# Twenty of the first FFN's 22 up tiles as seven half-width products, with the residual in DRAM and five queues in written order

## The chip, the cores and the metric

The kernel runs on one core of a Trainium2 chip. A core has five engines that each work through a queue of their own: TensorE (PE, matrix products; its loads of the stationary operand are listed apart as PEld), VectorE (DVE), ScalarE (ACT), GpSimd (POOL) and SyncE (SP, which here only issues DMA transfers; POOL issues some too). Working data lies in SBUF, results of matmuls in PSUM, inputs in DRAM. The metric is the device time of one execution in microseconds, as the median of several.

## The reference

Two layers of a transformer block. Layer 0 has a Fourier/Hyena mixer, layer 1 attention; both end in a convolutional FFN. Layer 0 works on 512 tokens x and on 256 context tokens ctx.

```python
def _conv_ffn(h, w_up, conv_w, conv_b, w_down):
    gate, val = jnp.split(h @ w_up, 2, axis=-1)          # h: tokens x 1024, w_up: 1024 x 5632
    return (jax.nn.silu(_dwconv3(gate, conv_w, conv_b)) * val) @ w_down   # 2816 -> 1024
...
x = x + g1 * yx                                          # yx: the mixer's output
x = x + g2 * _conv_ffn(_modulate(_rms_norm(x, norm2[i]), sh2, sc2), *ffn)
ctx = ctx + cg1 * yc
ctx = ctx + cg2 * _conv_ffn(_modulate(_rms_norm(ctx, norm2[i]), csh2, csc2), *ffn)
```

`_dwconv3` is a convolution of three taps along the tokens. The gains `g2`, shifts and scales come from `silu(c) @ w_mod + b_mod`, a vector by matrix product for each of the conditions.

## The kernel before

Features lie on the 128 partitions and tokens along the free axis. Targets and context stand side by side in one row of 772 columns: 512 targets, two zeros, 256 context tokens, two zeros, so that one convolution runs over both. A vector of 1024 features is eight such tiles. To keep float32 accuracy each operand is split into a rounded part and a rest, and each product is three matmuls (`mm3`, L194 to L198): high by high, high by rest, rest by high. ACT makes the high part (`hi`, L171), DVE subtracts it to give the rest (`lo`, L176). Weights come as 128 x 1024 tiles into the three buffers `wr` by SP's DMA and are split into `wh` and `wl`.

The first FFN is `ffn` (L1194 to L1251). The 2816 inner features are 22 tiles f. For each tile, `up(f)` loads a gate and a value weight, and runs 8 k tiles x 2 x 3 matmuls over 512 columns and as many over 260: 96 matmuls in all. Then come the convolution (`conv3`, L419 to L421, one ACT and two DVE operations), Silu (L1221), the product with the value half (L1223) and a split into `ah` and `al`. `fill` puts three of the vector by matrix products behind each tile from the third on (`gemv_dve`, a DVE multiply and sum of 128 x 1024, L282, and a small one, L283); 56 of them, with 80 DVE steps in all, fill DVE's free time in this FFN. The down product runs in groups of 8, 8 and 6 tiles (`GROUPS`), each by `res_proj` (L1148 on): eight output tiles m, each a sum over the group's k tiles, added to the residual `x` in SBUF by a DVE operation that scales it by the gain (L1189). The last group runs in two stages: first all eight m over the 512 target columns, then over the 260 others. The pieces of layer 1's first norm hang on these steps (`norm_hook`, L371): while the second stage runs on PE, DVE and ACT make the squares (L313) of the target columns, PE folds them over the partitions (L319) and spreads the result, and DVE and ACT scale the tiles. Layer 1's first product follows. An automatic scheduler orders this FFN on the engines.

Layer 1's FFN (`ffn_blocks`, L1795) already runs most of its tiles by Strassen's scheme: the k axis is halved and the columns are halved, so that gate and value tiles become a 2 x 2 block product done with seven products of half width, on sums of weight blocks (tiles `sum`, made by POOL DMAs, plain at L1872 and accumulating at L1874, and by DVE at L1878 and L1881). A table of step names, `UP_ORDER`, is the order of its queues. Each of its two sums has two buffers.

## Time and profile before

| | us |
|---|---|
| median of 3 runs | 1619.88 (1616.86 to 1622.33) |
| the profiled execution, its own time | 1611.81 |
| its span | 1610.0 |
| first FFN, from 377.00 to the last group's second stage at 917.85 | 540.85 |
| layer 1's FFN, 1262 to 1609 | 347 |

The mean granted TensorE clock of the profiled execution is 0.991. Rows of windows give, after the stretch and its length, the busy time and number of instructions of PE, PEld, DVE, ACT and POOL, then the granted clock, the mean busy share of the 16 DMA engines and GB/s. Rows of groups give line, engine, operation, output and inputs by the program's names, shape and count, then busy time and mean ns of one, then the engine's idle time before them and what ended it. Rows of the timeline give start, duration, engine and operation. A matmul's row is longer than the distance to the next start, since matmuls overlap in the array; the distance is what counts.

### The profile page before, as it was taken

The numbers are of one execution on the slowest core, as the hardware profiler recorded it, in microseconds if no ns is written. First come the engines' busy times: TensorE is split into PE (matmuls) and PEld (weight loads), VectorE is DVE, ScalarE is ACT, GpSimd is POOL, SyncE is SP. The second block draws the span as 40 slices with busy tenths as digits, with TensorE's granted clock in tenths as the row PEclk, the third lists the DMA queues.
The fourth block names the chain that finished last, engine by engine and source line by source line (L and its number), as shares of the span: only waits on it lengthen the run. The fifth ranks groups of instructions, "written<-read, shape, count | busy, mean of one in ns | idle before, by whom it ended". The sixth has DMA issues, their size and how long they took to land.

```text
span 1610.0 us, 22860 instructions
## 1 busy us (share of the span) xinstructions
PE 1560.5 (97%) x8968; PEld 1312.2 (82%) x8968; DVE 1173.2 (73%) x1963; ACT 671.8 (42%) x980; POOL 166.3 (10%) x245
## 2 busy tenths in 40 slices
PE   7999998999999999999999999999999999999998
PEld 5787887888888888888888887666648899999897
DVE  6789969878887354553354475799996899788784
ACT  4441234434232212321123244998883664444441
POOL 0022134000000000000000000122230022121110
PEclk9999999999999999999999998999999999999999
DMA  9336512533544244442343220000006266665543
GB/s 359 108 116 213 170 34 81 188 118 106 163 156 139 66 131 142 140 150 66 102 139 100 102 69 20 1 24 14 1 27 209 92 155 169 155 155 145 147 125 105
DMA packets 68121, 189.23 MB, mean 118 GB/s; under 512 B 7979, under 2 KB 15341, under 8 KB 66989
## 3 DMA queue, kind: packets, MB, share of 16 engines
q1 hardware_dynamic: 59053, 166.79, 31.6%
q0 software_dynamic: 8960, 20.98, 6.2%
q8 instruction: 70, 1.15, 0.3%
q14 instruction: 38, 0.31, 0.1%
HBM read 181.97 MB, written 5.77 MB: 117 GB/s over the span
## 4 chain that ended last, share of the span: by engine, by line
PE 76%; DVE 16%; issue 2%; ACT 2%; DMA 2%; POOL 1%; SPq 0%; DVEq 0%; ACTq 0%; POOLq 0%
PE mm L196 21%; PE mm L198 21%; PE mm L197 21%; DVE wl L176 2%; PE pv L1657 2%; DVE junk L282 2%; DVE S L1633 2%; PE s L1603 1%; DVE wr L1672 1%; PE ms L196 1%; PE ms L198 1%; PE ms L197 1%; DMA wr<-w_up 1%; POOL mx L1629 1%; PE mm L662 1%
## 5 line engine op out<-in xcount | busy, mean ns | idle before, releaser
L196 PE MATMUL mm<-hh,wh 128*128 128x512 f32 (+2 forms) x1192 | 395.6, 334 | 2.4 <-ACT hh L350 1.5
L197 PE MATMUL mm<-hl,wh 128*128 128x512 f32 (+2 forms) x1192 | 394.1, 331 | 2.4 <-DVE hl L359 2.3
L198 PE MATMUL mm<-hh,wl 128*128 128x512 f32 (+2 forms) x1192 | 393.9, 331 | 0.0
L171 ACT ACTIVATE wh<-wr 128x1024 fp32r<-128x1024 f32 (+3 forms) x187 | 177.9, 958 | 434.6 <-PE mm L197 393.4
L176 DVE TENSOR_TENSOR wl<-wr,wh 128x1024 fp32r<-128x1024 f32 (+3 forms) x187 | 207.3, 1114 | 121.6 <-ACT wh L171 121.0
L196 PEld LDWEIGHTS mm<-hh,wh 128*128 128x128 f32 x1192 | 225.4, 189 | 31.4 <-issue 2.4
L197 PEld LDWEIGHTS mm<-hl,wh 128*128 128x128 f32 x1192 | 225.4, 189 | 26.5 <-DVE hl L359 3.3
L198 PEld LDWEIGHTS mm<-hh,wl 128*128 128x128 f32 x1192 | 225.3, 189 | 21.8 <-DVE wl L176 0.4
L282 DVE SCALAR_TENSOR_TENSOR junk<-wr,sb 128x1024 bf16<-128x1024 f32 x128 | 156.2, 1220 | 44.8 <-DMA wr<-wmodT 44.5
L198 PE MATMUL mm<-ah,wl 128*128 128x512 f32 (+1 forms) x480 | 172.8, 360 | 0.4 <-DVE wl L176 0.4
L197 PE MATMUL mm<-al,wh 128*128 128x512 f32 (+1 forms) x480 | 171.9, 358 | 0.0
L196 PE MATMUL mm<-ah,wh 128*128 128x512 f32 (+1 forms) x480 | 171.4, 357 | 0.0
L1189 DVE SCALAR_TENSOR_TENSOR xr<-mm,mod,xr 128x512 f32<-128x512 f32 (+1 forms) x76 | 43.7, 594 | 88.7 <-PE mm L198 88.5
L198 PEld LDWEIGHTS mm<-ah,wl 128*128 128x128 f32 x480 | 90.3, 188 | 14.9 <-DVE wl L176 1.7
L197 PEld LDWEIGHTS mm<-al,wh 128*128 128x128 f32 x480 | 90.4, 188 | 13.6
L196 PEld LDWEIGHTS mm<-ah,wh 128*128 128x128 f32 x480 | 90.3, 188 | 13.6 <-ACT wh L171 0.5
L1657 PE MATMUL pv<-S,V 128*128 128x512 f32 x192 | 93.8, 598 | 2.5 <-ACT S L1636 2.5
L1611 ACT ACTIVATE S<-s,rks 128x512 f32<-128x512 f32 x96 | 62.6, 686 | 12.4 <-PE pv L1657 8.5
L412 POOL MEMSET kvh<- 128x2 f32 x1 | 0.1, 100 | 633.0 <-DVE nt L313 633.0
L1657 PEld LDWEIGHTS pv<-S,V 128*128 128x128 f32 x192 | 34.5, 190 | 34.8 <-issue 29.4
L1629 POOL PARTITION_ALL_REDUCE mx<-mx x16 | 44.9, 2804 | 164.6 <-DVE mx L1626 164.6
L171 ACT ACTIVATE wh<-sum 128x1024 fp32r<-128x1024 f32 x40 | 42.3, 1057 | 36.4 <-PE mm L197 13.9
(404 smaller groups left out, 3211.2 us busy)
## 6 DMA issues: line engine op xcount, KB each, us to landing
wr<-wmodT SPq DMA_DIRECT2D x80, 512.0 KB, 3.4
wr<-w_up SPq DMA_DIRECT2D x68, 512.0 KB, 3.4
sum<-w_up POOLq DMA_DIRECT2D x80, 256.0 KB, 4.6
wm<-wmod0a SPq DMA_DIRECT2D x8, 1024.0 KB, 10.5
wr<-w_in SPq DMA_DIRECT2D x16, 512.0 KB, 4.0
wr<-w_dn SPq DMA_DIRECT2D x16, 512.0 KB, 3.4
wr<-w_out SPq DMA_DIRECT2D x13, 512.0 KB, 3.5
wr<-w_o SPq DMA_DIRECT2D x11, 512.0 KB, 4.9
```

Of the source, the lines that this page charges most:

```text
L171: self.nc.scalar.activation(dst, src, AF.Copy)
L176: (eng or self.nc.vector).tensor_tensor(dst, src, hi.bitcast(F32), op=ALU.subtract)
L196: mmul(out, wh, xh, start=start, stop=False)
L197: mmul(out, wh, xl, start=False, stop=False)
L198: mmul(out, wl, xh, start=False, stop=stop)
L282: nc.vector.scalar_tensor_tensor(junk, raw, 1.0, self.sb[:, j, :], op0=ALU.mult, op1=ALU.mult, accum_out=acc)
L662: nc.tensor.matmul(ps[:, w], h3[r0 : r0 + 64, c : c + 128], self.w4[r0 : r0 + 64, w], start=True, stop=True)
L1189: nc.vector.scalar_tensor_tensor(x[m][:, a2:b2], ps[:, a2:b2], mod[:, 8 * sec + m, c : c + 1], x[m][:, a2:b2], op0=ALU.mult, op1=ALU.add)
L1611: nc.scalar.activation(c.S[a][j // 3][:, j % 3, :], c.ps[a, j], AF.Copy, scale=c.r[:, g : g + 1])
L1629: nc.gpsimd.partition_all_reduce(c.m[a][:, 1, :], c.m[a][:, 0, :], P, bass.bass_isa.ReduceOp.max)
L1633: v.tensor_tensor(c.S[a][h], c.S[a][h], mb.to_broadcast([P, 3, T]), op=ALU.subtract)
L1657: nc.tensor.matmul(c.P[a], V[:, j, o : o + 128], c.S[a][j // 3][:, j % 3, :], start=j == 0, stop=j == 5)
```

## The change

The first FFN gets its own function, `ffn_first`, whose order on all five queues is written out in a table (`UP0_ORDER`). Tiles 0 and 1 are computed whole, as before. Tiles 2 to 21 run by Strassen's scheme over the 772 columns: seven products P1 to P7, each four k tiles x 3 matmuls of 386 columns, 84 in all.

Their moving operands are two untouched quarters of the activations and four combinations T1 to T4 of the quarters, made once and split. Their stationary operands are the value weight, half of the gate weight, and two sums of weight blocks. For these, S1 issues four POOL DMAs per tile: two plain copies of a gate block and two that add a further block to it; S2 and S4 add the value blocks on DVE. Here each of the two sum tiles has one buffer. The seven results are put together by K1 (a copy by ACT) and seven DVE operations of 386 columns (C1, Ua, Xv, Ub, C2, C4, C3). Convolution, Silu, product and split (Ca, Cb, Cc, Si, Ml, Ah, Al) are as before.

The down product has six groups, of 4, 4, 4, 3, 3 and 4 tiles, since there are places for six split activation tiles only: four in the mixer's freed space and two in a later pool. The residual leaves SBUF: after the mixer's output product each residual tile is stored to DRAM (`xs`, by POOL); a down step D of the first five groups is scaled by ACT into a buffer `delta` (X, two pieces) and added to `xs` by an accumulating POOL DMA of 128 x 772 (Y). Before the last group the residual is loaded back by eight SP DMAs. The last group runs by `res_proj` in two stages as before, over 4 k tiles instead of 6, with all eight of its weights split ahead (Rk, Hk, Lk). The 80 vector by matrix steps stand singly in the table (G), their loads (Rm) among the weight loads.

Around it: the mixer's `x` tiles are reused as the residual, and their loads are issued by POOL and not SP; tile 0's products no longer begin among w_out's last ones; the second norm of layer 0 writes its scaled tiles to `u` and makes them high parts by one more ACT operation each; some small tiles have fewer buffers, and PSUM is opened anew around the FFN.

```diff
+UP0_ORDER = """
+S1.2 Rv2 Rm0 Rm1 S2.2 T1 G0 U1a T3 Ca0 Hv2 Cb0 Th3 T2 Ha2 Cc0 Th2 T4 Si0 Tl3 Th1.3 U1b Th1.0 Ml0 Th1.1 Th1.2 Tl1.3 Ah0 Tl2 Al0 Lv2 G1 Tl1.0 Tl1.1 Tl1.2
+P1.2 La2 Th4 G2 P2.2 K1.2 Tl4 P5.2 S4.2 Ca1 C1.2 Rv3 G3 Hb2 P6.2 Cb1 Rg2 Rm2 Lb2 Cc1 P7.2 S1.3 Hv3 Ua2 Si1 Lv3 Hg2 Ml1 P1.3 Lg2 Ah1 Xv2 G4 P4.2 K1.3
...
+UP0_GROUPS = ((0, 4), (4, 8), (8, 12), (12, 15), (15, 18), (18, 22))
...
-            nc.sync.dma_start(x[d][:, 0:512], I["xT"][d])
-            nc.sync.dma_start(x[d][:, C0 : C0 + C], I["cxT"][d])
+            nc.gpsimd.dma_start(x[d][:, 0:512], I["xT"][d])
+            nc.gpsimd.dma_start(x[d][:, C0 : C0 + C], I["cxT"][d])
...
+            if stage:
+                nc.gpsimd.dma_start(xs[m], x[m])
...
+        acts, keep = self.ffn_first(hh, hl, u, xs, first, rest.steps, gl1)
...
+        x = [self.t(self.xp, [P, TW], F32, f"xr{d}") for d in range(KD)]
+        for d in range(KD):
+            nc.sync.dma_start(x[d], xs[d])
...
-        self.ffn(0, x, hh, hl, TW, full, [[(0, 512)], [(512, 260)]], late, fill, ahook, early=True)
+        self.res_proj(0, 5, sh, sl, len(acts), None, x, late, ahook, keep, there=True)
...
+        def S1(f):
+            s = k_["sa", f], k_["sb", f] = [one1(tp_[0], 1024, f"sum{q}") for q in "ab"]
+            g, w = I["w_up"][i, f, 0], I["w_up"][i, f, 1]
+            for t_ in s:
+                nc.gpsimd.dma_start(t_[:, 512:1024], g[:, 0:512])
+            for t_, src in zip(s, (g[:, 512:1024], w[:, 0:512])):
+                nc.gpsimd.dma_start(t_[:, 512:1024], src, accum_op=ALU.add)
+
+        def S2(f):
+            s = k_["sa", f]
+            v.tensor_tensor(s[:, 0:512], s[:, 512:1024], k_["rv", f][:, 0:512], op=ALU.add)
...
+        def prod(ps, w, o, mov):
+            for q in range(4):
+                s = slice(o + 128 * q, o + 128 * q + 128)
+                self.mm3(ps[:, 0:N], w[0][:, s], w[1][:, s], *mov(q), q == 0, q == 3)
...
+        def C1(f):
+            k_["v", f] = two_(f, "fv")
+            plus(k_["v", f][:, 0:N], k_["t", f], k_["n", f])
...
+        def X(g, m):
+            k_["x", g, m] = self.t(hf2(), [P, TW], F32, "delta", 2)
+            for j, (o, (c, n)) in enumerate(zip("de", both)):
+                self.hi(k_["x", g, m][:, c : c + n], k_[o, g, m][:, 0:n], self.mod[i][:, 40 + m, j : j + 1])
+
+        def Y(g, m):
+            nc.gpsimd.dma_start(xs[m], k_["x", g, m], accum_op=ALU.add)
...
+        with self.tc.manual_schedule(engines={ENG.PE, ENG.DVE, ENG.Activation, ENG.SP, ENG.Pool}):
+            k_["wg", 0], k_["wv", 0] = first
+            take(KD)
+            Rv(1)
+            Rg(1)
+            Hv(1)
+            Hg(1)
+            U_(0, [(0, T)], (0, 1))
+            f2(False, 0)
+            U_(0, [(0, T)], (2, 3))
+            Lv(1)
+            f2(False, 1)
+            U_(0, [(0, T)], (4, 5, 6, 7))
...
+            U_(0, [(T, 260)], range(KD))
+            for s in UP0_ORDER.split():
+                step(s)
```

How the queues change. PE, one k tile of an up tile before (gate weight `wh_4479`, then value weight `wh_4485`; `hh` and `hl` are the split activations):

```order
L196 MATMUL mm_4489<-hh_598_3013,wh_4479 128x260
L197 MATMUL mm_4489<-hl_606_3021,wh_4479 128x260
L198 MATMUL mm_4489<-hh_598_3013,wl_4480 128x260
L196 MATMUL mm_4490<-hh_598_3013,wh_4485 128x512
L197 MATMUL mm_4490<-hl_606_3021,wh_4485 128x512
L198 MATMUL mm_4490<-hh_598_3013,wl_4486 128x512
L196 MATMUL mm_4490<-hh_598_3013,wh_4485 128x260
L197 MATMUL mm_4490<-hl_606_3021,wh_4485 128x260
```

and now, in the first product of tile 2:

```order
L239 MATMUL mm_4140<-hh_592_3009,wh_4034 128x386
L240 MATMUL mm_4140<-hl_600_3017,wh_4034 128x386
L241 MATMUL mm_4140<-hh_592_3009,wl_4035 128x386
L239 MATMUL mm_4140<-hh_593_3010,wh_4034 128x386
L240 MATMUL mm_4140<-hl_601_3018,wh_4034 128x386
L241 MATMUL mm_4140<-hh_593_3010,wl_4035 128x386
```

Every matmul of a tile has the same width now, and there are 84 for 96.

DVE among the seven products of tile 2, with tile 1's convolution and product and a gemv step between them (`suma`, `sumb` are the weight sums, `t`, `fv`, `fg` the combinations, `fq` the convolution):

```order
L1420 TENSOR_TENSOR sumb_3955<-suma_3954,wr_3960 128x512
L1471 TENSOR_TENSOR fv_4204<-t_4177,mm_4164 128x386
L320 SCALAR_TENSOR_TENSOR junk_4208,gacc_4209<-wr_3964,sb_82 128x1024
L321 TENSOR_TENSOR mod_4_73<-gacc_4209,pcol_67 128x1
L1513 SCALAR_TENSOR_TENSOR fq_4201<-mm_3975,pcol_67,fq_4201 128x511
L1513 SCALAR_TENSOR_TENSOR fq_4201<-ms_3977,pcol_67,fq_4201 128x259
L219 TENSOR_TENSOR wl_4213<-sumb_3955,wh_4212 128x1024
L1518 SCALAR_TENSOR_TENSOR fq_4201<-mm_3975,pcol_67,fq_4201 128x511
L1518 SCALAR_TENSOR_TENSOR fq_4201<-ms_3977,pcol_67,fq_4201 128x259
L1471 TENSOR_TENSOR t_4177<-t_4177,mm_4140 128x386
L219 TENSOR_TENSOR wl_4255<-wr_4206,wh_4254 128x1024
```

Sums, combinations and splits of sums are new on DVE; the conv steps, splits and gemv steps stood there before.

POOL where the first down group meets the weight sums (the queue was empty here before):

```order
L1411 DMA suma_897_4692<-w_up 128x512
L1411 DMA sumb_898_4693<-w_up 128x512
L1413 DMA suma_897_4692<-w_up 128x512
L1413 DMA sumb_898_4693<-w_up 128x512
L1586 DMA xs0_584_2969<-delta_917_4798 128x772
L1586 DMA xs1_585_2970<-delta_929_4862 128x772
L1411 DMA suma_944_4916<-w_up 128x512
L1411 DMA sumb_945_4917<-w_up 128x512
L1413 DMA suma_944_4916<-w_up 128x512
L1413 DMA sumb_945_4917<-w_up 128x512
```

The residual's accumulations (L1586) stand between the sums of one tile and the next in one queue.

More of the change, by code (lines that the diff above doesn't have):

```diff
@@ L482, in mixer @@
         self.S2 = self.pool("S2", bufs=19)
-        xp = self.pool("xp", side="right")
+        xp = self.x0pool = self.pool("xp", side="right")
         self.pf = self.pool("pf")
         self.wm = self.pool("wm", bufs=2)
+        cT = self.t(self.wm, [P, KD, 2], F32, "cT", 1)
+        nc.sync.dma_start(cT, I["cT"])
+        self.sT = self.t(self.wm, [P, KD, 32], F32, "sT", 1)
+        v.memset(self.sT, 0.0)
+        nc.scalar.activation(self.sT[:, :, 0:2], cT, AF.Silu)
         hp = self.pool("hp", side="right")
@@ L1253, in layer0 @@
     def layer0(self):
         nc, I = self.nc, self.I
-        yh, yl, pre = self.mixer()
+        yh, yl, pre, x = self.mixer()
+        hp = self.pool("h2p")
+        hf = self.pool("hf")
         nt = self.pool("nt", bufs=5)
-        hp = self.pool("h2p")
-        self.xp = self.pool("xres")
-        tp = lambda: self.t(nt, [P, 512], F32, "nt")
-        x = [self.t(self.xp, [P, TW], F32, f"xr{d}") for d in range(KD)]
+        dy = self.pool("dy", space=bass.MemoryType.DRAM)
+        xs = [self.t(dy, [P, TW], F32, f"xs{d}") for d in range(KD)]
@@ L1270, in layer0, with norms @@
         self.zero_pads(hh + hl)
-        norms = lambda i, k: self.norm_hook(self.norm(i, k, x, hh, hl, 0, T, tp), self.norm(i, k, x, hh, hl, C0, C, tp))
-        nhook, rest = norms(0, 1)
+        u = [self.t(hf, [P, TW], F32, f"u{d}") for d in range(KD)]
+        for t_ in u:
+            nc.gpsimd.memset(t_[:, 512:514], 0.0)
+            nc.gpsimd.memset(t_[:, 770:772], 0.0)
+        def norms(i, k, x, pool, whole):
+            tp = lambda: self.t(pool, [P, 512], F32, "nt")
+            return self.norm_hook(*[self.norm(i, k, x, hh, hl, c0, n, tp, whole and whole(c0, n)) for c0, n in ((0, T), (C0, C))])
+        nhook, rest = norms(0, 1, x, nt, lambda c0, n: lambda d: u[d][:, c0 : c0 + n])
         gl = self.gl0
+        first = []
         def hook(stage, j, m):
```

382 lines of the change are left out of this document (297 added, 85 removed).

## The prediction

> **What bounds the kernel now.** I read the busy times and the chain of waits of the page first, then the table of windows over the first FFN, the rows by form of its matmuls, and the same table for layer 1's FFN, which is the nearest thing in this trace to what the change builds.
>
> ```profile
> span 1610.0 us, 22860 instructions
> PE 1560.5 (97%) x8968; PEld 1312.2 (82%) x8968; DVE 1173.2 (73%) x1963; ACT 671.8 (42%) x980; POOL 166.3 (10%) x245
> PE 76%; DVE 16%; issue 2%; ACT 2%; DMA 2%; POOL 1%; SPq 0%; DVEq 0%; ACTq 0%; POOLq 0%
> ...
> 450.00:550.00 100.00, 100.00 (x569) 87.29 (x568) 65.81 (x108) 25.94 (x28) 0.00 (x0) 1.00 0.38 125
> 740.00:850.00 110.00, 110.00 (x626) 96.14 (x625) 45.97 (x69) 20.01 (x21) 0.00 (x0) 1.00 0.33 107
> 377.00:917.85 540.85, 540.73 (x3024) 469.63 (x3024) 297.05 (x472) 129.19 (x146) 0.00 (x0) 1.00 0.38 121
> ```
>
> PE is 97% busy and carries 76% of the chain. In the windows (length, then busy time and instructions of PE, weight loads, DVE, ACT and POOL, then granted clock, DMA share, GB/s) the first FFN has no idle PE at all: 540.73 of 540.85 us, at clock 1.00, with DVE at 55% (297.05) and the DMA engines at 0.38. So there a matmul removed is time removed, and there is room under PE for more work of DVE and DMA, on average. A busy PE need not be PE at its peak, so the spacing matters:
>
> ```profile
> 401.52 0.39 PE L198 MATMUL mm<-hh,wl 128*128 128x512 f32 x1
> 401.75 0.28 PE L196 MATMUL mm<-hh,wh 128*128 128x260 f32 x1
> 401.87 0.29 PE L197 MATMUL mm<-hl,wh 128*128 128x260 f32 x1
> ```
>
> Starts are 0.23 us apart behind 512 columns and 0.12 behind 260: the rate is that of the columns (0.45 ns each), with nothing else in it.
>
> **The matmuls: -42.2 us.** An up tile was 2 x 8 x 3 x (512 + 260 columns) = 96 matmuls of mean width 386; a Strassen tile is 7 products x 4 k tiles x 3 = 84 of exactly 386. From the window 450 to 550, 100 us / 569 = 0.1757 us for a mean of 386 columns; since the cost follows the columns, a 386 wide matmul should cost the same. 20 tiles x 12 x 0.1757 = 42.2 us off. [...]
>
> ```profile
> L196 PEld LDWEIGHTS mm<-hh,wh 128*128 128x128 f32 x1192 | 225.4, 189 | 31.4 <-issue 2.4 <-ACT hh L350 1.7 <-ACT wh L171 1.1
> ```
>
> I take 0.1757, because in today's stream the same 189 ns loads hide behind 260 column matmuls 0.12 us apart. [...]
>
> **DVE: +6 us, in the first tiles only.** What DVE does per tile is new, and priced by these rows (line, operation, shapes, count, then busy time, mean ns):
>
> ```profile
> L282 DVE SCALAR_TENSOR_TENSOR junk<-wr,sb 128x1024 bf16<-128x1024 f32 x80 | 97.8, 1222 | 44.5 <-DMA wr<-wmodT 44.2
> L176 DVE TENSOR_TENSOR wl<-wr,wh 128x1024 fp32r<-128x1024 f32 x57 | 69.5, 1219 | 97.2 <-ACT wh L171 97.2
> L1223 DVE TENSOR_TENSOR fg<-fg,mm 128x772 f32<-128x772 f32 x22 | 21.0, 955 | 6.8 <-ACT fg L1221 6.8
> L1932 DVE TENSOR_TENSOR t<-t,mm 128x256 f32<-128x256 f32 x40 | 16.7, 418 | 5.6 <-PE mm L198 5.5
> L1881 DVE TENSOR_TENSOR sum<-sum,wr 128x512 f32<-128x512 f32 x20 | 13.8, 689 | 0.1
> ...
> 404.92 1.22 DVE L282 SCALAR_TENSOR_TENSOR junk<-wr,sb 128x1024 bf16<-128x1024 f32 x1
> 406.26 1.22 DVE L282 SCALAR_TENSOR_TENSOR junk<-wr,sb 128x1024 bf16<-128x1024 f32 x1
> 409.74 1.23 DVE L176 TENSOR_TENSOR wl<-wr,wh 128x1024 fp32r<-128x1024 f32 x1 [2.06 <-ACT wh L171]
> 410.88 1.02 DVE L420 SCALAR_TENSOR_TENSOR fg<-mm,pcol,fg 128x771 f32<-128x771 f32 x1
> ```
>
> The next operation starts some 0.08 us before a row ends, so in a queue 1024 columns cost 1.14 us, a gemv step with its small operation 1.34, 772 columns 0.87, 512 columns 0.60, and 386, between the rows of 256 and 512, 0.47. A Strassen tile costs DVE 3 splits of 1024 (3.4), one of 512 (0.6), 2 weight sums (1.2), 7 combinations of 386 (3.3), 4 of 772 (3.5): 12 us against 14.8 us of PE (84 x 0.1757). The 80 gemv steps (107 us) and the down splits come on top. By the written order, from tile 0's context columns to tile 5's last product, DVE has: 28 combinations 13.2, the transforms T1 to T4 with their splits 32 x 0.47 = 15.0, 13 splits of 1024 14.8, 4 gate splits 2.4, 10 sums 6.0, 12 conv steps 11.0, 10 products and activation splits 8.7, 16 gemv steps 21.4, 2 down splits 1.2: 93.7 us. PE has 48 x 0.12 + 96 x 0.1757 for tile 1, 4 x 14.8 and two down steps of 24 matmuls: 90.3 us. DVE is the longer by 3, and comes to it with the norm of the target columns still in hand; I take +6. Lower bound 0 (if gemv steps fall into its waits only), upper 14 (no overlap of the transforms with PE: 15 less what tile 1 covers). Later the ratio falls: 141 of 175 us for tiles 6 to 12, 99 of 120 for 13 to 17, 62 of 84 at the end, so no further term.
>
> **The junction of w_out and the FFN: +1 us.** Today tile 0's first products stand among w_out's last; now the two follow each other and each norm piece has one more ACT operation. The rows give 0.6 to 1 us per operation of a piece, so 0 to 3.
>
> **DMA: +4 us.** Loads and accumulations run on two kinds of queue:
>
> ```profile
> q1 hardware_dynamic: 59053, 166.79, 31.6%
> q0 software_dynamic: 8960, 20.98, 6.2%
> ```
>
> Packets, MB, and share of 16 engines' span: 166.79 MB in 0.316 x 1610 us is 0.328 MB/us, and 20.98 in 0.062 x 1610 is 0.210. In the new FFN 56.6 MB come by hardware (172 us), 21 MB of weight sums by software (100 us) and 40 accumulations Y of 395 KB into DRAM (15.8 MB, 75 us at the same rate): 347 of some 515 us. The densest place is tiles 13 to 17, where 26 of the 56 gemv loads stand: 20.5 MB by hardware and 10.8 by software, 114 us of transfers in 120 us of PE. That is 95%, above any stretch of today, and late loads stall DVE there and then PE. I take 4; lower 0, upper 20 (rival b).
>
> **The end of the FFN: +5 us.** The last group has 4 k tiles instead of 6. Its second stage is cover for the norm of the target columns:
>
> ```profile
> 917.85 0.28 PE L196 MATMUL mm<-ah,wh 128*128 128x260 f32 x1
> ...
> 939.94 0.39 PE L198 MATMUL mm<-hh,wl 128*128 128x512 f32 x1
> 943.09 0.61 PE L319 MATMUL ms<-ones,nt 128*128 128x1 f32 x4 [2.75 <-DVE nt L313]
> 943.55 0.48 PE L196 MATMUL mm<-hh,wh 128*128 128x512 f32 x1
> ...
> 917.85:937.40 19.55, 19.53 (x162) 19.20 (x161) 17.15 (x38) 10.21 (x16) 0.19 (x4) 1.00 0.25 78
> ```
>
> The norm's sum is ready 943.09 - 917.85 = 25.2 us after the stage starts; PE waits for it 2.75 us today. The stage has 162 matmuls in 19.55 us and becomes 8 x 4 x 3 = 96 of the 260 kind and the same 18 others, 13.6 us. The chain on DVE loses one split of 768 columns (0.95). So the wait grows to 2.75 + 19.55 - 13.6 - 0.95 = 7.8, 5 more. Bounds 3 (DVE earlier by the lighter queue) and 8 (nothing lighter).
>
> **The rest: 0.** The residual's way back is 8 loads of 395 KB on SP, behind one w_qa load that waits for the seventh of the last eight down splits: 1.2 us each at 0.328 MB/us plus 3.4 to land, needed one per 12 x 0.23 = 2.8 us of PE, three PSUM buffers deep, so hidden; if the w_qa load holds them, up to 6. The x loads that move from SP to POOL lie beside the mixer, on an engine that is busy 10% of the span: 0 to 2. ACT gains X, two pieces per down step, and starts from 129.19 us of 540.85 in the window above.
>
> **Sum.** -42.2 + 6 + 1 + 4 + 5 = -26 against the profiled execution (1611.81 us, span 1610.0). The median of the runs, 1619.88, stands 8.1 above it; I carry the difference over: 1619.88 - 26 = 1593 us, rounded down.
>
> **The rivals.** (a) *DVE and the norm are covered.* Layer 1's Strassen FFN, with DVE at 92% in its first window, loses little PE time:
>
> ```profile
> 1290.00:1400.00 110.00, 106.72 (x799) 100.48 (x798) 101.53 (x166) 58.19 (x80) 22.41 (x32) 1.00 0.62 160
> 1262.00:1609.00 347.00, 338.89 (x2339) 312.67 (x2338) 287.09 (x464) 160.80 (x229) 51.81 (x72) 1.00 0.53 140
> ```
>
> Then only the last group's wait stays: -42 + 4, 1582 us. Against it: DVE's sum above exceeds PE's. (b) *The DMA engines become the bound in tiles 13 to 17.* An accumulation reads and writes its target; if Y costs twice its bytes' time, the densest place has 14 x 1.9 = 26 us more, 140 us in 120: about 16 above the forecast, 1609. For it: today's stretches never pass 0.62. (c) *Slower: the weight sums come late.* Layer 1 has two buffers for each sum; the new tile has one, so tile f+1's sum starts only when Lb of tile f has read it.
>
> ```profile
> L1872 POOL DMA_DIRECT2D sum<-w_up x40: 547/566/1137, 1201.5 to 1537.9; - x40
> L1874 POOL DMA_DIRECT2D sum<-w_up x40: 850/880/1123, 1205.7 to 1542.4; - x40
> ...
> DMA to landing us min/median/max: 3.0/4.6/7.1
> ```
>
> Issue 0.57 and 0.88, landing 4.6, then sum 0.69, split 1.06 and 1.22: about 9.5 us to the first sum's weights, 12 at the longest landing, in a period of 14.8 us without down steps. If Y transfers before it in POOL's queue and full engines push landing past 12 us the tile waits: at 14 us 3.4 us per tile, 68 us, 1661. For it: one buffer, two kinds of accumulation on one queue. Against it: the slack of 5 us, and 8.4 us more of down steps in most tiles. [...]
>
> **Numbers.** Forecast 0.50 (1585 to 1600 as its own range), (a) 0.22, (b) 0.17, (c) 0.11. The range 1578 to 1613 takes in (a), (b) and the terms' bounds, and leaves (c) out. A change of 0.3% (4.9 us) is what this kernel's measurement can tell. Faster by more: 0.87, from the first two whole and most of (b); within it 0.03, the far end of (b); slower 0.10, (c).
>
> **What would show it.** Starts of 386 column matmuls 0.175 us apart; 20 x 84 of them. PE idle in the first 90 us after the context columns, ended by DVE. A DMA share above 0.8 in tiles 13 to 17, and DVE or ACT waiting for weight loads there. A wait of about 8 us before attention's norm fold, ended by DVE. It is wrong if PE waits for the weight sums or their splits in every tile (c), if 386 columns cost 0.19, or if the residual's loads hold the last group.

## The result and the profile after

The changed kernel takes 1607.27 us (median; 1603.81 to 1611.15), the kernel before in the same session 1617.49 (1613.53 to 1622.33). The ratio is 0.9935, 95% interval 0.9914 to 0.9956: about 10 us faster, where 26 were forecast. The sign was right and the time lies in the range, but more than half of the expected gain did not come.

Busy times, chain and queues on the page of the changed kernel (queues: packets, MB, share of 16 engines' span; the last row gives an issue's line, engine and count, KB each and us to landing):

```profile
span 1602.0 us, 23289 instructions
PE 1534.1 (96%) x8728; PEld 1321.0 (82%) x8728; DVE 1304.3 (81%) x2212; ACT 770.1 (48%) x1177; POOL 272.9 (17%) x421
q1 hardware_dynamic: 62365, 161.18, 30.4%
q0 software_dynamic: 25344, 64.08, 19.7%
PE 41%; DVE 17%; DMA 8%; issue 3%; ACT 2%; POOL 1%; SPq 0%; DVEq 0%; ACTq 0%; POOLq 0%
xs<-delta POOLq DMA_DIRECT2D x40, 386.0 KB, 6.2
```

The span fell by 8.0 us, not by 42: there are 240 matmuls fewer, and PE is now idle where it was not. Its share of the chain of waits went from 76 to 41%, and DMA's from 2 to 8%. The windows of the changed kernel say where. The last two of them, attention and layer 1's FFN, were touched by none of the terms of the sum:

```profile
400.00:450.00 50.00, 45.98 (x252) 43.26 (x251) 49.70 (x91) 23.00 (x36) 5.79 (x8) 0.97 0.40 105
450.00:700.00 250.00, 247.82 (x1397) 234.44 (x1396) 209.42 (x348) 105.13 (x151) 47.81 (x63) 1.00 0.78 191
550.00:600.00 50.00, 50.00 (x285) 46.85 (x284) 36.37 (x64) 18.52 (x30) 10.59 (x14) 1.00 0.89 203
700.00:850.00 150.00, 141.03 (x774) 132.23 (x773) 117.31 (x194) 60.02 (x89) 29.89 (x40) 0.99 0.84 219
750.00:800.00 50.00, 45.57 (x249) 41.60 (x249) 34.67 (x63) 17.09 (x28) 10.31 (x13) 0.99 0.97 253
...
900.00:916.70 16.70, 15.86 (x60) 12.79 (x61) 10.96 (x16) 6.32 (x9) 0.00 (x0) 0.85 0.72 280
916.70:938.50 21.80, 16.95 (x126) 15.56 (x124) 18.90 (x44) 9.24 (x18) 0.19 (x4) 1.00 0.36 113
938.50:1247.40 308.90, 301.88 (x1420) 210.22 (x1421) 260.31 (x422) 224.35 (x363) 54.82 (x31) 0.98 0.14 44
1247.40:1598.00 350.60, 345.98 (x2366) 317.85 (x2364) 289.69 (x470) 163.25 (x231) 51.77 (x72) 1.00 0.52 139
```

Those two stretches of the kernel before:

```profile
943.10:1258.90 315.80, 305.04 (x1421) 213.22 (x1422) 260.45 (x422) 224.71 (x363) 54.45 (x31) 0.97 0.14 44
1258.90:1606.00 347.10, 341.99 (x2366) 315.76 (x2364) 288.25 (x469) 162.16 (x231) 51.81 (x72) 1.00 0.53 141
```

The window 550 to 600 is the yardstick: PE never idle, 50 us / 285 = 0.1754 us a matmul. That is the pace of the kernel before (100 us / 569 = 0.1757, so 284.5 matmuls in 50 us), and what other windows lack of it is lost time: 400 to 450 has 252, which is 5.7 us; 450 to 700 has 1397 of 1422.5, 4.5 us; 700 to 850 has 774 of 853.5, 14.0 us. Counting matmuls is better here than reading PE's busy time, which shows only 9 of the 14, since a slow matmul still counts as busy: from 799.18 to 802.40 those of 386 columns start 0.32 us apart instead of 0.175, with rows of 0.53 us instead of 0.34, and the first one behind a wait has a row of 0.44 or 0.45 us.

| stretch | forecast | measured |
|---|---|---|
| up to the last group's second stage (917.85 before, 916.70 now) | -25.4 | -1.2 |
| that stage, up to attention's norm fold | -0.8 | -3.5 |
| attention | 0 | -6.9 |
| layer 1's FFN | 0 | +3.5 |

So 24 us went missing in the first of them, which is the FFN and what stands ahead of it, and the last three brought net 6 more than forecast. The first row is good to 2 or 3 us only: w_out's last product, just ahead of the FFN, starts at 374.97 us in this execution and at 373.1 to 377.7 us in those of the changed kernel's variants below. The experiments take the stretches in turn.

### The profile page after: what moved, and what is told of

The parts are those of the page before. It is cut to its first block, busy times and chain, and to the rows that moved or that the text cites. A ratio compares the mean times of both kernels' runs of the same rounds, so it can differ in the third digit from the quotient of the medians.

```text
span 1602.0 us, 23289 instructions
## 1 busy us (share of the span) xinstructions
PE 1534.1 (96%) x8728; PEld 1321.0 (82%) x8728; DVE 1304.3 (81%) x2212; ACT 770.1 (48%) x1177; POOL 272.9 (17%) x421
## 3 DMA queue, kind: packets, MB, share of 16 engines
q1 hardware_dynamic: 62365, 161.18, 30.4%
q0 software_dynamic: 25344, 64.08, 19.7%
## 4 chain that ended last, share of the span: by engine, by line
PE 41%; DVE 17%; DMA 8%; issue 3%; ACT 2%; POOL 1%; SPq 0%; DVEq 0%; ACTq 0%; POOLq 0%
PE mm L239 9%; PE mm L241 9%; PE mm L240 9%; DMA wr<-wmodT 4%; DVE junk L320 3%; DVE wl L219 2%; PE pv L1999 2%; PE ms L239 2%; PE ms L240 2%; PE ms L241 2%; DVE S L1975 1%; DMA wr<-w_up 1%; DMA suma<-w_up 1%; PE s L1945 1%; DVE wr L2014 1%
## 5 line engine op out<-in xcount | busy, mean ns | idle before, releaser
L214 ACT ACTIVATE wh<-wr 128x1024 fp32r<-128x1024 f32 (+4 forms) x185 | 157.4, 860 | 234.6 <-PE mm L240 128.4
L239 PE MATMUL mm<-hh,wh 128*128 128x256 f32 (+3 forms) x696 | 231.9, 333 | 4.6 <-ACT wh L214 1.8
L241 PE MATMUL mm<-hh,wl 128*128 128x256 f32 (+3 forms) x696 | 229.2, 329 | 5.9 <-DVE wl L219 5.9
L240 PE MATMUL mm<-hl,wh 128*128 128x256 f32 (+3 forms) x696 | 230.3, 331 | 2.5 <-DVE hl L397 2.3
L219 DVE TENSOR_TENSOR wl<-wr,wh 128x1024 fp32r<-128x1024 f32 (+4 forms) x185 | 182.7, 993 | 27.6 <-ACT wh L214 27.4
L239 PEld LDWEIGHTS mm<-hh,wh 128*128 128x128 f32 x696 | 133.4, 192 | 17.4 <-ACT wh L214 2.3
L241 PEld LDWEIGHTS mm<-hh,wl 128*128 128x128 f32 x696 | 132.8, 191 | 16.8 <-DVE wl L219 8.6
L240 PEld LDWEIGHTS mm<-hl,wh 128*128 128x128 f32 x696 | 133.2, 191 | 13.2 <-DVE hl L397 3.3
L239 PE MATMUL ms<-hh,wh 128*128 128x386 f32 (+2 forms) x240 | 76.7, 319 | 1.9 <-DVE fg L1474 1.2
L1586 POOL DMA_DIRECT2D xs<-delta x40 | 34.1, 853 | 203.8 <-ACT delta L216 201.3
L239 PE MATMUL mm<-x,wh 128*128 128x512 f32 x192 | 65.3, 340 | 0.0
L240 PE MATMUL mm<-x,wh 128*128 128x512 f32 x192 | 65.2, 339 | 0.0
```

Source lines behind the costliest of these rows:

```text
L214: self.nc.scalar.activation(dst, src, AF.Copy)
L219: (eng or self.nc.vector).tensor_tensor(dst, src, hi.bitcast(F32), op=ALU.subtract)
L239: mmul(out, wh, xh, start=start, stop=False)
L240: mmul(out, wh, xl, start=False, stop=False)
L241: mmul(out, wl, xh, start=False, stop=stop)
L1586: nc.gpsimd.dma_start(xs[m], k_["x", g, m], accum_op=ALU.add)
```

## The experiments

**The middle of the FFN: loads or DVE?** The table of waits of the changed kernel (who waits for whom: us in all, times, longest), PE, DVE and ACT from 376 to 920:

```profile
PE mm L241 <- DVE wl L219: 8.1, 7, 2.3
...
DVE junk L320 <- DMA wr<-wmodT: 21.2, 17, 3.4
...
DVE suma L1417 <- DMA suma<-w_up: 10.2, 5, 3.5
...
ACT wh L214 <- DMA wr<-w_dn: 63.0, 13, 9.3
```

PE waits for the rest of a split (DVE), DVE for gemv loads and for weight sums, ACT for down weights. Two kernels take one side each out of the 80 steps G.

`g_no_load`:

```diff
-            k_["rm", i_, jt] = self.wraw(I["wmodT"][i_, jt])
+            k_["rm", i_, jt] = self.sb[:, 0, :]
```

> The changed kernel with the 56 loads of the vector by matrix products left out of the first FFN: each step multiplies a tile that stays in SBUF, so its values are not the reference's; DVE's instructions are the same. Theory A (late weight loads through three shared buffers stall DVE and then PE in tiles 12 to 17): the some 14 us lost between 700 and 850 us go, and a few of the first tiles' with them; about 15 us shorter than the changed kernel, some 1592. Rival B (DVE's own work is the bound): no more than 3 us shorter. Rival C (the accumulations and the weight sums fill the DMA engines by themselves): 4 to 8 us shorter.

`g_no_dve`:

```diff
-            self.gemv_dve(i_, jt, (c,), k_["rm", i_, jt])
+            v.tensor_tensor(self.mod[i_][:, jt, c : c + 1], k_["rm", i_, jt][:, 0:1], self.col(f"bm_{i_}", jt), op=ALU.add)
```

> The changed kernel with the 80 DVE multiplies of 128 x 1024 replaced by additions of one column that still read the loaded tile, so the products are not computed; all loads stay, in the same order and buffers. If DVE's work is the bound in the first tiles, the some 10 us lost between 376 and 450 us go, and tiles 12 to 17 keep their 14: about 10 us shorter, some 1597. If the late loads are the whole cause: 0 to 3 us shorter. If DVE's work is the cause in both places: 20 or more shorter.

They took 1590.16 and 1590.67 us (ratios 0.9828, 0.9809 to 0.9847, and 0.9831, 0.9805 to 0.9857), and they win them in different places. Windows of the one without loads:

```profile
400.00:450.00 50.00, 45.96 (x250) 43.03 (x249) 49.70 (x90) 22.81 (x36) 5.80 (x8) 0.97 0.30 73
700.00:850.00 150.00, 150.00 (x851) 144.40 (x850) 123.94 (x203) 65.08 (x95) 31.44 (x55) 1.00 0.63 136
```

and of the one without the wide multiplies:

```profile
400.00:450.00 50.00, 50.00 (x288) 48.25 (x287) 47.50 (x85) 26.76 (x40) 6.35 (x9) 1.00 0.47 127
700.00:850.00 150.00, 144.86 (x806) 138.38 (x805) 95.19 (x152) 64.11 (x94) 29.60 (x53) 0.99 0.78 201
```

The first tiles (400 to 450) lose their time to DVE's multiplies: without loads nothing changes there (250 matmuls, DVE 49.70 of 50 us), without the multiplies all of it comes back (288). Tiles 13 to 17 (700 to 850) lose theirs to the loads: it is gone without them (851), and more than half is still there (806, 8 us) when DVE is a fifth lighter (95.19 us against 117.31) but the loads come. The expectation for `g_no_dve` had all 14 us stay, so the multiplies, which also hold the buffers of their loads, have a part in it.

**Bytes, or buffers?** The forecast had reckoned the bytes of that place, 114 us in 120. The rates came out as forecast: from the queue rows above, 161.18 MB in 0.304 x 1602 us is 0.331 MB/us by hardware, 64.08 in 0.197 x 1602 is 0.203 by software. The landing of a load did not. The rows of the weight tile `wr` from 700 to 850, in the kernel before (the row for all its loads alone) and then in the changed one (count, ns at least, at the median and at most, first and last start; the last row is again for all loads):

```profile
DMA to landing us min/median/max: 3.0/3.3/4.7
```

```profile
L320 DVE SCALAR_TENSOR_TENSOR junk<-wr,sb x24: 1217/1220/1226, 699.6 to 818.7; 128x1024 bf16<-128x1024 f32 x24
...
L214 ACT ACTIVATE wh<-wr x20: 507/526/1065, 700.5 to 846.2; 128x384 fp32r<-128x384 f32 x11, 128x1024 fp32r<-128x1024 f32 x7, 128x512 fp32r<-128x512 f32 x2
L219 DVE TENSOR_TENSOR wl<-wr,wh x20: 549/559/1226, 705.0 to 848.3; 128x384 fp32r<-128x384 f32 x11, 128x1024 fp32r<-128x1024 f32 x7, 128x512 fp32r<-128x512 f32 x2
...
DMA to landing us min/median/max: 1.9/5.2/7.6
```

With the DMA share at 0.84 and not 0.33 (740 to 850 before), the median landing is 5.2 us and not 3.3, although many of the loads are smaller now. All loads go through three buffers `wr`, and a buffer is tied up from issue to the end of its last reader: for a gemv load 5.2 + 1.22 (DVE's multiply) = 6.4 us, for a full weight 5.2 + 1.07 (ACT's high part) + 1.23 (DVE's rest) = 7.5 us, before any turn in the queues of ACT and DVE. By the written order tiles 13 to 17 issue 49 loads in some 120 us of PE, so a buffer has 3 x 120 / 49 = 7.3 us. Such a ring has little slack, and none where a reader is late. But the DMA engines are not free there either: from 750 to 800 their share is 0.97, and 6.2 of the 14 us go in that third. Two kernels test which of the two it is, buffers or bytes: both leave out the 40 accumulations, and the second has a fourth buffer, at the same bytes.

```diff
-            nc.gpsimd.dma_start(xs[m], k_["x", g, m], accum_op=ALU.add)
+            pass
...
+        ring, at = [self.t(self.W, [P, 1024], F32, "wr") for _ in range(3)], [0]
...
+            if False and late and len(ring) < 4:
...
+            if True and late and len(ring) < 4:
+                at[0] %= 3
+                ring.insert(at[0], one1(hf2(), 1024, "wr3"))
```

> The changed kernel without the 40 accumulating transfers Y into DRAM, so the first five down groups are missing from the residual; ACT's scaling stays and writes PSUM in place. The three weight buffers are held through the FFN and used in turn, the order of the loads is the same. If the accumulations crowd the DMA engines (they are 15.8 of some 93 MB): landings between 700 and 850 us fall from 5 to 6 us to about 4, and of the 14 us lost there under 5 stay. If three buffers are too few even without them: 8 or more stay.

> The same without the transfers Y, with a fourth weight buffer in the place of the two tiles that Y would read. Loads, bytes and order are those of the kernel with three. If the number of buffers is what bounds: of the loss between 450 and 850 us in the kernel with three, at least two thirds go. If the bytes bound: the same loss, within 2 us.

They took 1590.29 us with three buffers (ratio 0.985, 0.9832 to 0.9867) and 1589.88 with four (0.9829, 0.9799 to 0.986). The window of three, then of four:

```profile
700.00:850.00 150.00, 146.03 (x810) 138.57 (x809) 119.33 (x195) 61.00 (x91) 19.07 (x26) 0.99 0.63 181
```

```profile
700.00:850.00 150.00, 149.12 (x844) 143.33 (x843) 122.64 (x202) 64.65 (x94) 19.86 (x42) 1.00 0.63 178
```

Leaving the accumulations out takes away almost half of the loss (14.0 to 7.6 us, between the two guesses), with the median landing down from 5.2 to 4.3. At the same DMA share of 0.63 the fourth buffer then takes three quarters of the rest away (844 matmuls, 1.7 us lost). Over 450 to 850, the stretch named beforehand, the loss falls from 10.5 to 4.4 us, a little less than the two thirds that were asked for. So without Y's traffic it is mostly the number of buffers that binds, and not the bytes.

How Y costs the other half is not shown. Without Y the landings are shorter and the engines are no longer full. DVE's wait for weight sums, which stand behind Y in POOL's queue, also falls, from 6.5 to 1.4 us in this stretch, while its wait for gemv loads does not (7.0 and 8.4). What a fourth buffer does with the accumulations in place was not tried.

The totals of the two kernels are alike because the 6 us are lost again further on. With four buffers PE stands 2.1 us at the residual's reload, with three it does not, and the way from the last group's first product to attention's norm fold takes 48.0 us with four and 44.1 with three; layer 1's FFN takes another 3 us more in the execution with four.

**Steps placed anew.** `g_spread` writes the table anew so that 4 of the 16 gemv steps stay ahead of tile 6, and 20 loads instead of 26 fall in tiles 13 to 17. The steps are also taken in another order, which is the part of the edit printed here:

```diff
-        gl1 += [(1, jt, j) for jt in range(48) for j in ((0, 1) if jt < 16 else (0,))]
+        gl1 += [(1, jt, j) for k in range(16) for jt in (16 + 2 * k, k, 17 + 2 * k) for j in ((0, 1) if jt < 16 else (0,))]
```

> The changed kernel with the 80 vector by matrix steps and their 56 loads placed anew in the table, nothing added or left out: 4 of 16 steps stay ahead of tile 6 (the rest follow just ahead of the down steps that need them), 20 loads of 26 in tiles 13 to 17, 6 of 2 behind, and rows with two steps alternate with rows that have one. If DVE's work is the bound in the first tiles: the some 10 us lost up to 450 us shrink to 2 or 3. If the loads' density is what stalls tiles 12 to 17: the 14 us lost between 700 and 850 us halve. Together 12 to 16 us shorter, some 1593. Rival (three buffers are too few at any density): tiles 6 to 12, which get eight loads more, lose what the others gain, within 5 us of the changed kernel.

It is slower than the kernel before: 1632.92 us, ratio 1.0097 (1.0074 to 1.012). Its windows:

```profile
400.00:450.00 50.00, 50.00 (x288) 48.29 (x287) 46.95 (x76) 26.67 (x40) 6.33 (x9) 1.00 0.34 90
450.00:700.00 250.00, 236.34 (x1294) 222.91 (x1293) 195.61 (x329) 94.15 (x138) 45.60 (x59) 0.97 0.75 190
700.00:850.00 150.00, 138.07 (x731) 128.27 (x730) 116.38 (x194) 57.70 (x88) 27.53 (x36) 0.94 0.79 198
```

The first tiles are mended (288), but 450 to 850 loses 44 us instead of 18.5: PE is idle for 25.6 of them, and the lower granted clock (0.97 and 0.94) makes some 16 more. Neither guess on record had a loss. Per matmul DVE has as much to do as in the changed kernel (195.61 us / 1294 against 209.42 / 1397 from 450 to 700), and the DMA share is no higher. What changed is where the loads stand in the ring of three: tiles 6 to 12 now have 27 gemv loads where they had 19, tiles 13 to 17 have 20 for 26. The waits from 450 to 850 of this kernel:

```profile
PE mm L241 <- DVE wl L219: 8.0, 4, 4.1
...
DVE junk L320 <- DMA wr<-wmodT: 21.7, 15, 5.6
```

DVE's wait for gemv loads is as long in sum as in the changed kernel (21.7 and 21.2 us), but the longest is 5.6 us and not 3.4, and PE's longest wait for a split is 4.1 us. My reading is that the splits behind a late load in DVE's queue reach PE late, so that an order which balances work but not the life of the buffers makes it worse. No run tests that by itself: tiles 13 to 17 have fewer loads than before and lose more (22 us), so the count of loads alone does not explain it.

**The end of the FFN.** The timeline of the changed kernel at the residual's reload (start, duration, engine, line, operation; the bracket is the wait ahead of it), and below it the rows of the tile `xr` (count, ns at least, at the median and at most, first and last start; the landing of its loads):

```profile
900.84 0.79 PE L239 MATMUL mm<-x,kh 128*128 128x512 f32 x1 [4.91 <-DVE xr L1232]
901.43 0.63 PE L240 MATMUL mm<-x,kh 128*128 128x512 f32 x1
901.86 0.63 PE L241 MATMUL mm<-x,kl 128*128 128x512 f32 x1
...
905.14 0.39 PE L240 MATMUL mm<-x,kh 128*128 128x512 f32 x1
905.37 0.40 PE L241 MATMUL mm<-x,kl 128*128 128x512 f32 x1
...
L1298 SPq DMA_DIRECT2D xr<-xs x8: 319/397/550, 891.3 to 897.9; - x8
L1232 DVE SCALAR_TENSOR_TENSOR xr<-mm,mod,xr x4: 743/744/750, 900.0 to 905.8; 128x512 f32<-128x512 f32 x4
...
DMA to landing us min/median/max: 7.4/8.1/9.4
```

The first of the eight loads is issued at 891.3. Ahead of it in SP's queue stand the last down weights, each of which waits for a `wr` buffer (the eighth is issued at 890.3), and then one w_qa load (890.9). The eight loads take 8.1 us at the median to land, where the weights take 5.2 in the densest stretch. DVE adds the first product at 900.0; by then the three PSUM buffers are full and PE has stood for 4.9 us. Behind the stall the matmuls of 512 columns start 0.43 us apart instead of 0.23, ten of them until 905.14, and the window's granted clock is 0.85: 2.0 us more. Two kernels: `six_psum` gives the last group six PSUM buffers of 512 columns, `xr_early` puts the reload into the table among the last weight loads.

```diff
-        self.close("psA")
-        self.ps = self.pool("psA", space=PSUM)
-        self.mmw = 1024
...
+                        self.mm3(ps[:, a - z : a + n - z], wh[:, w], wl[:, w], src_h[k][:, a : a + n], src_l[k][:, a : a + n], k == 0, k == nk - 1)
```

> The changed kernel with the last down group's products in PSUM tiles of 512 columns, six deep, where they are of 1024 columns, three deep. Theory (PE stops at the fourth product since the residual's reload is late): the wait of 5.1 us at 895 us and the 2 us of slow clock behind it go, 7 us shorter, some 1600. Rival (the norm behind it is late by the same reload): the wait before the norm's fold grows by what is saved, within 2 us of the changed kernel.

```diff
-Hk4 Y4.7 Lk4 Hk5 Lk5 Rk7 Hk6 Lk6 Hk7 Lk7
+Hk4 Y4.7 Q0 Lk4 Hk5 Q1 Lk5 Rk7 Q2 Q3 Hk6 Lk6 Q4 Q5 Hk7 Lk7 Q6 Q7
...
+        def Q(m):
...
+                for d in (5, 0, 1, 2, 3, 6, 7, 4):
+                    xr[d] = self.t(self.xp, [P, TW], F32, f"xr{d}")
+            nc.sync.dma_start(xr[m], xs[m])
```

> The changed kernel with the residual's eight loads issued in the written order between the last down weights, ahead of the load of w_qa, and into places in an order by which the first free ones are used first. Theory (the late reload holds DVE's chain of residual, squares and norm, which sets the end of the FFN): the first residual operation starts 2 to 4 us earlier, the wait of 5.1 us shrinks by as much, and attention's norm fold comes 2 to 4 us earlier; some 1604. Rival (the last down weights, which DVE splits in the same queue, come later by what the residual gains): within 1.5 us.

`six_psum` took 1610.94 us (0.9978, 0.9959 to 0.9996): no gain, and less of one than the changed kernel has (0.9935). Its window at the reload is full, but its waits show where the time went:

```profile
850.00:900.00 50.00, 50.00 (x268) 45.68 (x267) 28.12 (x41) 21.18 (x34) 6.31 (x23) 1.00 0.61 150
...
PE mm L239 <- DVE nt L390: 7.1, 1, 7.1
...
PE k L239 <- DVE pt L1728: 3.4, 1, 3.4
```

PE runs ahead of the reload and then waits 7.1 us for the norm, whose pieces DVE can make only once the residual is there; the fold comes at 939.7 us against 938.5. `xr_early` moves that chain itself:

```profile
L1232 DVE SCALAR_TENSOR_TENSOR xr<-mm,mod,xr x5: 745/746/752, 896.3 to 904.7; 128x512 f32<-128x512 f32 x5
```

DVE adds the first product at 896.3 instead of 900.0, PE's wait for it falls from 4.9 to 0.9 us, and attention's norm fold comes at 933.7 instead of 938.5 with tile 2 starting at the same time. The time is 1603.22 us (0.9922, 0.9894 to 0.9951). That is 4 us under the changed kernel's median, but the kernel before was also 2.6 us faster in that session, and by the ratios (0.9922 and 0.9935) the totals cannot be told apart; the gain is seen in the trace alone. What sets the end is when the residual reaches DVE; buffers on PE's side only move the wait.

**Attention, 6.9 us shorter.** It computes the same as before. The kernel before has a wait there that the changed one lacks, `PE k <- DVE pt` of 3.4 us (in `six_psum`, which opens the PSUM pool later, it is back). `before_psum_reopened` is the kernel before with its PSUM pool opened anew ahead of the last group:

```diff
             if gi == 2 and early:
+                self.close("psA")
+                self.ps = self.pool("psA", space=PSUM)
```

> The kernel before, with PSUM closed and opened anew ahead of the last down group, as the changed kernel does; nothing else. Theory (attention's first query product got another PSUM place, which is free earlier): the wait of 3.4 us at 980 us and the slow clock behind it go, 6 to 7 us shorter than the kernel before. Rival (attention gained by something else in the change, the earlier reload or other SBUF places): within 1.5 us of the kernel before.

It took 1615.61 us (0.9991, 0.9979 to 1.0003). Its attention, and a wait in its FFN:

```profile
953.80:1262.30 308.50, 301.41 (x1420) 210.10 (x1421) 261.34 (x422) 224.74 (x363) 54.52 (x31) 0.99 0.15 46
...
PE mm L196 <- DVE fg L421: 3.6, 1, 3.6
```

Attention falls from 315.8 to 308.5 us and the wait is gone. It is no chance of one execution: the eleven kernels here that open the pool ahead of the last group take 307 to 311 us from fold to fold, `before` and `before_layout`, which do not, 315.8 and 313.9. As I read it, opening the pool anew turns the order of PSUM places, so that the tile that waited no longer shares a place with a product that DVE reads late; the trace shows the wait, not the places. The wait is half of the 6.9 us; the mean granted clock of the stretch goes with the rest (0.97 before, 0.98 and 0.99 now), which was not taken apart further. The same kernel pays about as much in its FFN, where PE waits 3.6 us at the new opening, for DVE's last operation on an old tile, so its total stands still.

**Layer 1's FFN, 3.5 us longer at the same instructions.** `aligned` makes the one tile that had shrunk to a column 64 bytes wide again, so that the tiles behind it start at multiples of 64:

```diff
-        self.ones32 = self.t(p, [P, 1], F32, "ones32")
+        self.ones32 = self.t(p, [P, 16], F32, "ones32")
```

> The changed kernel with the tile of ones 16 columns wide where the change made it 1 (only its first column is used): the tiles behind it, the weight buffers and layer 1's activations among them, then start at multiples of 64 bytes again, as before the change, where in the changed kernel they start 32 bytes off. Theory (TensorE reads operands that start 32 bytes off 64 more slowly: 256 column matmuls of layer 1's FFN stand 117 to 118 ns apart in the changed kernel and 113 to 114 before): back to 113 to 114 ns, layer 1's FFN 4 to 5 us shorter, the first FFN some 2; about 6 us shorter in all, some 1601. Rival (the pace is the clock's or the traffic's doing): 117 to 118 ns stay, within 2 us of the changed kernel.

It took 1606.31 us (0.994, 0.9918 to 0.9961) and the stretch kept its 350.70 us, with starts still 117 to 118 ns apart, so that theory falls. `combo` joins it with `g_spread` and `xr_early`:

> The three edits together: the vector by matrix steps placed anew, the residual's loads early, and the tiles at multiples of 64 bytes. If their causes are separate the gains add up: 6 + 3 + 14, some 1584. Rival (one wait takes the place of another): not under 1595.

It took 1627.42 us, 1.0067 (1.0048 to 1.0085): 5.5 us under `g_spread`, about what the earlier reload saves in the trace, and with the loss of `g_spread` in it. Then the opposite way, the kernel before with nothing but the change's smaller tiles, which puts layer 1's tiles at the changed kernel's SBUF addresses:

```diff
-        self.ones32 = self.t(p, [P, 32], F32, "ones32")
+        self.ones32 = self.t(p, [P, 1], F32, "ones32")
...
-        i0 = self.t(pool, [P, 24], I32, "rq_i")
+        i0 = self.t(pool, [P, 24], I32, "rq_i", 1)
...
+        cT = self.t(self.wm, [P, KD, 2], F32, "cT", 1)
...
+        self.sT = self.t(self.wm, [P, KD, 32], F32, "sT", 1)
```

> The kernel before with the change's small SBUF edits alone: a tile of ones of one column, two condition tiles moved to the mixer's weight pool, one buffer each for the small tiles of the inverse root. The weight buffers and all of layer 1's FFN then stand at the very addresses of the changed kernel, and the program is otherwise that of the kernel before. Theory (the places in SBUF set TensorE's pace, in a way that neither a shift to multiples of 64 bytes nor one of the moving tiles alone undoes): layer 1's FFN takes 350 to 351 us where it takes 347, 3 to 4 us longer than the kernel before. Rival (the pace comes with something else of the change, its longer program or its traffic): 347 us, within 1.5 us of the kernel before.

It took 1622.6 us, 1.0052 (1.0033 to 1.0071): 7.5 us slower than the kernel before, with the same work, where 3 to 4 were expected. Its window, and the first and last of 36 steps in a full run of its 256 column matmuls:

```profile
1260.20:1612.40 352.20, 347.67 (x2364) 320.65 (x2364) 289.69 (x468) 162.32 (x231) 51.88 (x72) 0.99 0.52 138
...
1341.72 0.28 PE L198 MATMUL mm<-th,wgl 128*128 128x256 f32 x1
...
1345.96 0.28 PE L198 MATMUL ms<-th,wl 128*128 128x256 f32 x1
```

The same in the kernel before, 36 steps from such a run:

```profile
1339.77 0.28 PE L198 MATMUL mm<-hh,wl 128*128 128x256 f32 x1
...
1343.85 0.28 PE L198 MATMUL mm<-th,wl 128*128 128x256 f32 x1
```

4.24 us against 4.08: 117.8 ns from start to start against 113.3, with PE never idle. The stretch has 1776 such matmuls; some (those with `wgh` and `wgl`) stand at 120 ns in both kernels, and the stretch as a whole is 5.1 us longer. Where the other 2.4 us of the total went was not looked for. `before_psum_reopened`, which has the old places, keeps 113 to 114 ns. `xr_early_pad` puts unused bytes ahead of layer 1's tiles, so that all but the weight buffers lie where they lay before:

```diff
+        self.t(self.pool("pad"), [P, 392], F32, "pad")
```

> The kernel xr_early with 1568 unused bytes ahead of layer 1's FFN tiles, so that all but the weight buffers stand at the addresses of the kernel before. Theory (the place of the moving operands sets the pace): 256 column matmuls of layer 1's FFN go from 117 to 118 ns back to 113 to 114, 4 to 5 us shorter than xr_early, some 1599. Rival (it is the place of the weight buffers, or none of both): 117 to 118 ns stay, within 1.5 us.

It took 1602.12 us (0.9925, 0.9905 to 0.9945), not to be told from `xr_early`; these two are the fastest that compute all. The pace was not restored:

```profile
1242.60:1596.00 353.40, 348.45 (x2366) 320.10 (x2364) 290.43 (x470) 163.10 (x231) 51.88 (x72) 1.00 0.52 138
```

So the small tiles' edits set this pace, without any other part of the change. Which address does it stays open: neither a start at a multiple of 64 bytes nor the old places of the tiles other than the weight buffers brought it back, which leaves the weight buffers' own places as a guess that was not tried.

## Why the prediction was right and where it was wrong

**What bounds the kernel.** Right for the kernel before: where PE stayed fed, each matmul removed was time removed (285 of them in 50 us from 550 to 600, 284.5 before).

**The matmuls.** Right: 0.1754 us a matmul in a full window, down steps included, against 0.1757. The loads of the stationary operand stay hidden (from 550 to 600 they take 46.85 us beside PE's 50.00).

**DVE in the first tiles, +6.** Right in place, cause and size: 5.7 us from 400 to 450, and `g_no_dve` shows that they are DVE's. Another 3.3 us went from 376 to 400, where the forecast had 1 for the junction with w_out, and these have another cause:

```profile
379.25 0.75 PE L241 MATMUL mm<-hh,wl 128*128 128x512 f32 x1 [1.17 <-DVE wl L219]
379.80 0.63 PE L239 MATMUL mm<-hh,wh 128*128 128x512 f32 x1
```

PE waits 1.17 us for a split, and the six matmuls behind it start 0.43 us apart instead of 0.23; the granted clock from 376 to 400 is 0.93. `g_no_dve` has that wait too (1.2 us), and `xr_early`, with the same work for DVE, has it as well (1.16 us), but neither has the slow matmuls behind it. From w_out's last product to tile 2's first it takes 39.5 us here and 37.0 in both of them: most of this loss comes and goes between executions, and it is not the gemv steps'.

**DMA, "I take 4".** Here the forecast failed, in the size of this term. Tiles 13 to 17 lost 14.0 us and tiles 6 to 12 another 4.5, 18.5 for 4. The step priced transfers by bytes over rate, and the rates were right. What it left out is that the loads share three buffers, so that a load's price is the time its buffer is tied up, and that this time grows with the traffic (landing 3.3 to 5.2 us). Without any gemv load the 14 us were gone (`g_no_load`). With the 40 accumulations Y left out, 7.6 us of the 14.0 stayed, and three quarters of these went with a fourth buffer at the same traffic; by which way Y costs the other 6 us is open. The prediction set its 95% against "today's stretches never pass 0.62"; that holds for the windows that it shows, but the first 40 us of the kernel before stand at 0.94.

**Rival (b)** came near the measured time, 1609 for 1607, and that is luck: it had 16 us more in this place alone, and none of the other stretches. The engines did come close to full there (0.97 from 750 to 800), but not for its reason, an accumulation at twice its bytes' time. From 700 to 850 the software queue moves 12.35 MB in 42.4% of the time with Y and 7.08 MB in 22.0% without, so Y's part is 5.27 MB in 30.6 us, 0.172 MB/us: some 1.2 times the time at 0.210.

**The end of the FFN, +5.** The wait at the norm fold is there, ended by DVE, 4.6 us instead of 7.8:

```profile
PE ms L357 <- DVE nt L351: 4.6, 1, 4.6
```

So the stretch became shorter by 3.5 us, not 0.8: the term is 2.3 and not 5, a little under the lower bound of 3 (DVE earlier by the lighter queue). It is no gift of the stall at the reload: `xr_early`, which has almost none, waits the same 4.6 us.

**"The rest: 0", with the residual's way back "up to 6" if the w_qa load holds it.** The residual did come late. With 4.9 us of wait and 2.0 of slow matmuls it cost 7, just past that bound. The w_qa load is only the last of what held it: it is issued 0.6 us behind the eighth down weight, and all of these wait for `wr` buffers. The other part is landing, 8.1 us at the median where the prediction reckoned with 3.4. The condition was named and given no chance of its own.

**Rival (a)** asked that DVE be covered; it was not. **Rival (c)** did not come: DVE waits 10.2 us for weight sums in five places, not in each of 20 tiles, and PE keeps its full pace from 550 to 600.

**What no term had.** Attention -6.9 us, half of it a wait of 3.4 us that is also gone in `before_psum_reopened`; layer 1's FFN +3.5, where the small tiles' edits alone bring 5.1 (`before_layout`). They cancel in part, so the total hides them; without the table by stretches the shortfall would have read as 18 us (26 less the span's 8), where the stretch up to the last stage alone has 24.

The sum with measured sizes, for the FFN up to the last stage: -36.4 of the matmuls (the other 5.8 of the 42.2 lie in that stage) + 5.7 + 3.3 + 18.5 + 7 = -1.9, measured -1.2.

## What to carry to other kernels

Price a load that goes through shared buffers by how long a buffer is tied up (landing under the traffic it will have, plus its readers) against buffers x time / loads (here 6.4 to 7.5 us against 7.3), and only then by bytes; and look for the densest 50 us, where the engines may be full although the mean leaves room (here 0.97 from 750 to 800, 0.78 from 450 to 700). When a value that the last stage needs goes out to DRAM and back, look at what stands ahead of its load in the issuing queue and how long it takes to land, and move the load before adding buffers behind it (here the norm's fold came at 933.7 us in `xr_early` and at 939.7 in `six_psum`, against 938.5). Compare two kernels stretch by stretch, those that the change does not touch too: here a pool opened at another point took 7.3 us from attention (`before_psum_reopened`), and small tiles of another size added 5.1 to layer 1's FFN (`before_layout`).

## What the runs showed of the hardware that was not expected

- 256 column matmuls of layer 1's FFN start 113.3 ns apart in `before` and 117.8 in `before_layout`, the same instructions with a few small tiles made smaller or moved, and with them the places of layer 1's tiles in SBUF; which place does it is open.
- Behind an idle stretch of 4.9 us PE ran at about half its pace: 512 columns 0.43 us apart instead of 0.23, for ten matmuls, with 4.3 us from the first of them (900.84) to the first at full pace (905.14). At 379.25 us the same pace follows a wait of only 1.17 us, and in `xr_early` it does not follow the same wait (1.16 us), so the length of the wait alone does not set it.
- The median landing of the loads into `wr` went from 3.3 to 5.2 us as the DMA share went from 0.33 to 0.84, while over the whole span the bytes per time of busy engines stayed almost as they were (0.33 MB/us by hardware, 0.21 and 0.20 by software). Accumulating 386 KB into DRAM landed in 6.2 us at the median.
